# Router of a two-branch decoder layer with experts: squares beside the additions, a shorter root, second choice by weights, ranks as two sums, fewer fillers

## The chip, the cores and the metric

The kernel runs on one core of one Trainium2 chip. The metric is the device time of a launch in microseconds, as the median of several runs. A profile is of one execution; its own time stands beside the medians.

## What is computed

One layer for 256 tokens of width 2048, float32. A mixer (a state-space branch and an attention branch, gated and added) gives `x`; then a router picks for each token one of 4 groups and two of its 8 experts, and 32 experts of width 512 do their part:

```python
x = x + merged @ w_out[l]
h2 = rms_norm(x, ffn_norm_g[l])

g_prob = softmax(t @ rg_w + rg_b)                      # 4 groups, top 1
g_top, g_idx = lax.top_k(g_prob, 1)
e_logits = (t @ re_w + re_b).reshape(n_tok, 4, 8)[arange(n_tok), g_idx[:, 0]]
e_prob = softmax(e_logits)                             # 8 experts, top 2
e_top, e_idx = lax.top_k(e_prob, 2)
e_top = e_top / sum(e_top)
gate = g_top * e_top
for e in range(32):
    hid = silu(t @ w_gate[e]) * (t @ w_up[e])
    out = out + combine[:, e:e + 1] * (hid @ w_down[e])
```

## The kernel before

**Stages.** Up to some 625 us the kernel computes the mixer: weight blocks of 128 x 1024 are loaded (`raw`), split into a rounded part and a rest (`wh`, `wl`), and multiplied in three products each. The last four blocks are the output projection `wout`; `out_fin(n)` adds its result to `x2` (512 columns, two token halves t = 0 and 1), `x2_tr` transposes `x2` on TensorE (TensorE writes `bga`, ScalarE copies it to `xt2`) and takes the squares for the norm (`junk`, sums in `ssq`), `route_mm` multiplies with the router's weights (`wrg`). Transposes and router products are put off by some turns (`later`), so they come between the products of the next block; behind the last block (n = 3) they stand bare.

**Router.** Behind the last block come fillers, transposes of the identity that nobody reads (`keep_busy`, counts in `WARM`), then on VectorE the norm `r2` (`rsqrt`: ScalarE's root, a reciprocal and one Newton step), the logits `lgs`, and `first_max`: the maximum, a mask of those equal to it, the mask weighted with 8 to 1 (`desc`), the maximum of that, and a mask of the first. It is done for the experts of every group (`oh1`) and for the groups (`oh_g`, spread as `ohb`), in turns; then again for the second choice (`oh2`) with the first masked off (`el2`). `R1`, `R4` and `R32` (one name, `R`, in the profile, with 128x2, 128x8 and 128x64 elements) hold these values. A sum over the tokens (TensorE, with a triangle of ones `ult` and with `ones`) gives each token its rank in its expert (`rk`, in `bgb`), and from it the slot `slotv`.

**Experts.** An expert takes up to 32 tokens. For four experts at a time `gather` builds a selection (`EQ`, scaled as `SL`) and multiplies `x2` with it into `XB` (part of the tile `XY`); for the first four it is cut into pieces between the products of expert 0. `gate_up` uses four 2 MB pieces of weights (`ew`), `down` two. 192 pieces go through a ring of 11, later 10, buffers: `load_piece` issues the next when a buffer is free. Seven pieces are issued during the output projection, one near its end, three as soon as the mixer's buffers are free; every further one follows the use of a piece:

```python
            used[0] += 1
            load_piece()
```

**Order.** Each engine runs its instructions in the order in which the code issues them; nothing reorders them. All loads of weights are issued by SP, one queue, and a load that waits for its buffer holds up those behind it. Compute calls go through a helper, so all have line L77 in the profile; tiles tell them apart. Constants lie in one pool (`cp`), allocated ahead of the mixer's buffers and of three of the ring's.

Of the kernel before, what the change touches and what calls it, by code (L numbers as in the profile page):

```python
# [9 lines left out]
F32 = mybir.dt.float32  # L10
F32R = mybir.dt.float32r
I32 = mybir.dt.int32
AF = mybir.ActivationFunctionType
OP = mybir.AluOpType
# [3 lines left out]
P = 128  # L18
T = 256
D = 2048  # L20
EPS = 1e-6
# [17 lines left out]
LSPLIT = 512  # L39
NEG = -1.0e30  # L40
MAGIC = 12582912.0
WARM = (36, 8)


class Meter:
# [37 lines left out]
def hybrid_block(ctx, tc, A, out):  # L83
    nc = tc.nc
    load = {"vec": 0.0, "act": 0.0, "pe": 0.0}
    vec = Meter(nc.vector, load, "vec")
    act = Meter(nc.scalar, load, "act")
# [8 lines left out]
    def slot(h, shape, dt, name):  # L96
        return hp.tile(shape, dt, name=name, tag=f"h{h}")
# [13 lines left out]
    def bg_tile(k):  # L111
        return pbg.tile([P, 512], F32, name="bg" + "ab"[k], tag="bg" + "ab"[k])
# [66 lines left out]
    pool.iota(eidx, pattern=[[1, 1]], base=0, channel_multiplier=1, allow_small_or_imprecise_dtypes=True)  # L179
    iotan = cp.tile([P, 32], F32, name="iotan")  # L180
    vec.tensor_scalar(iotan, iota, -BIG, None, op0=OP.add)
    desc = cp.tile([P, 8], F32, name="desc")
    vec.tensor_scalar(desc, iota[:, 0:8], -1.0, 8.0, op0=OP.mult, op1=OP.add)

    def rsqrt(y, v, t):
        act.activation(t, v, AF.Sqrt)
        vec.reciprocal(y, t)
        vec.tensor_tensor(t, y, y, op=OP.mult)
        vec.tensor_tensor(t, t, v, op=OP.mult)
        vec.tensor_scalar(t, t, -0.5, 1.5, op0=OP.mult, op1=OP.add)  # L190
        vec.tensor_tensor(y, y, t, op=OP.mult)
# [173 lines left out]
    def out_fin(n):  # L365
        def f(a):
            c = slice(512 * n, 512 * n + 512)
            x2 = S["x2"]
            if n == 0:
                S["xt2"] = {}  # L370
                S["lg"] = [bg_tile(1), bg_tile(1)]
            for t in range(2):
                vec.tensor_tensor(x2[:, t, c], x2[:, t, c], a[t], op=OP.add)
            for t in range(2):
                later(D_X2 if n < 3 else 1, lambda t=t: x2_tr(n, t))
            for t in range(2):
                later(D_ROUTE if n < 3 else 2, lambda t=t: route_mm(n, t))
        return f

    def x2_tr(n, t):  # L380
        ps = bg_tile(0)
        for i in range(4):
            k = 4 * n + i
            pe.transpose(ps[:, P * i:P * i + P], S["x2"][:, t, P * k:P * k + P], ident)
        xt = S["xt2"][n, t] = slot((2 * n + t) % 4, [P, 4, P], F32, "xt2")
        act.copy(xt, ps.rearrange("p (i c) -> p i c", i=4))
        junk = slot(4 + (2 * n + t) % 4, [P, 512], F32, "junk")
        xs = S["x2"][:, t, 512 * n:512 * n + 512]
        if n < 3:
            act.activation(junk, xs, AF.Square, accum_out=ssq[:, t, n:n + 1])  # L390
            if n == 2 and t == 1:
                act.activation(tiny, ones[:, 0:1], AF.Sqrt)
        else:
            vec.scalar_tensor_tensor(junk, xs, 1.0, xs, op0=OP.mult, op1=OP.mult, accum_out=ssq[:, t, n:n + 1])
# [576 lines left out]
    def keep_busy(n):  # L971
        ps = acc_tile()
        for _ in range(n):
            pe.transpose(ps[:, 0:P], ident, ident)

    keep_busy(WARM[0])
    r2 = cp.tile([P, 4, 2], F32, name="r2")
    vec.tensor_reduce(r2[:, 0], ssq, axis=AX.X, op=OP.add)
    vec.tensor_scalar(r2[:, 1], r2[:, 0], 1.0 / D, EPS, op0=OP.mult, op1=OP.add)
    rsqrt(r2[:, 2], r2[:, 1], r2[:, 3])  # L980
    rs2 = r2[:, 2]
    lg = rt.tile([P, 2, 36], F32, name="lgs")
    for t in range(2):
        vec.scalar_tensor_tensor(lg[:, t], S["lg"][t][:, 0:36], rs2[:, t:t + 1], rbias, op0=OP.mult, op1=OP.add)
# [3 lines left out]
    OV = rt.tile([32, 35], F32, name="OV")  # L988
    oli = rt.tile([1, 33], I32, name="oli")

    def first_max(oh, x, m, one, wide):
        n, bc = x.shape[-1], lambda a: a.to_broadcast(list(x.shape))
        ds = desc[:, None, None, 8 - n:8] if wide else desc[:, None, 8 - n:8]
        ex = lambda a: bc(a[:, :, :, None] if wide else a[:, :, None])
        vec.tensor_reduce(m, x, axis=AX.X, op=OP.max)
        yield
        vec.tensor_tensor(oh, x, ex(m), op=OP.is_equal)
        yield
        vec.tensor_tensor(oh, oh, bc(ds), op=OP.mult)
        yield  # L1000
        vec.tensor_reduce(one, oh, axis=AX.X, op=OP.max)
        yield
        vec.tensor_tensor(oh, oh, ex(one), op=OP.is_equal)
        yield

    gl = lg[:, :, 0:4]
# [8 lines left out]
            lambda: act.activation(gx, gx, AF.Exp),  # L1015
            lambda: vec.tensor_tensor(oh1, oh1, ohb, op=OP.mult)]
    vec.scalar_tensor_tensor(el2, oh1, NEG, el, op0=OP.mult, op1=OP.add)
    for i, _ in enumerate(first_max(oh2, el2, m2, R4[:, 4], True)):
        if i < len(side):
            side[i]()  # L1020
    vec.tensor_tensor(oh2, oh2, ohb, op=OP.mult)
    dif, w1, w2_ = R4[:, 5], R4[:, 6], R4[:, 7]
    vec.tensor_tensor(R32[:, 3], oh1, oh2, op=OP.add)
    vec.tensor_tensor(dif, m2, m1, op=OP.subtract)
    act.activation(dif, dif, AF.Exp)
    M = R32[:, 3].rearrange("p t g e -> p t (g e)")
    rk = bg_tile(1)
    pe.matmul(rk[:, 0:64], ult, R32[:, 3].rearrange("p t g e -> p (t g e)"), start=True, stop=False)
    pe.matmul(rk[:, 32:64], ones, M[:, 0], start=False, stop=True)
    keep_busy(WARM[1])  # L1030
    gsum = R1[:, 1]
    vec.tensor_reduce(gsum, gx, axis=AX.X, op=OP.add)
    rank = rk[:, 0:64].rearrange("p (t e) -> p t e", t=2)
# [258 lines left out]
```

## Time and profile before

| | us |
|---|---|
| Median of 3 runs | 1555.99 (1554.79 to 1556.02) |
| The profiled execution | 1556.73 |
| Its span, first to last instruction | 1555.0 |
| TensorE busy in the span | 1256.5 (81%) |
| VectorE busy | 541.9 (35%) |
| ScalarE busy | 450.9 (29%) |
| Chain that ended last: DMA, TensorE, VectorE, ScalarE | 51%, 46%, 2%, 1% |

The shares are means over two stages that have different limits, so they are read by stretch: the mixer up to 625 us, the router up to 635 us, the experts behind it. A timeline row gives start, duration and the idle time of the engine before it with what ended it; "x2" after a shape counts instructions merged into the row. A float32 matmul stands as two instructions there.

### The profile page before, as it was taken

Reading aid. Unit: us, or ns where it says so; the run is one execution under the profiler, and the core shown is the slowest. Engines: PE = TensorE matmul, PEld = TensorE weight load, DVE = VectorE, ACT = ScalarE, POOL = GpSimd, SP = SyncE. Lnnn points to the kernel's source line nnn. Section 1 sums busy time; section 2 is a strip of 40 time slices with the busy share of each in tenths; the row PEclk is TensorE's granted clock in tenths of the full one; section 3 lists DMA queues with packets and bytes.
Section 4 is the critical chain, followed back from the end, with each engine's and each line's share of the span. In section 5 each row is a group of like instructions: output and inputs, shape, how many; then the busy total and the mean of one; then the engine's idle time right before and its main releaser. Section 6 shows DMA issues by size and latency. Waiting matters only on the chain.

```text
span 1555.0 us, 25114 instructions
## 1 busy us (share of the span) xinstructions
PE 1256.5 (81%) x10646; PEld 857.4 (55%) x10646; DVE 541.9 (35%) x1346; ACT 450.9 (29%) x768; POOL 49.4 (3%) x105
## 2 busy tenths in 40 slices
PE   9999999999999999878558558558657657657697
PEld 8888888888878888644224224224224223324364
DVE  7846787898866644302002002002002002002001
ACT  5654576644454444211101101100110110110101
POOL 6600000000000000000000000000000000000000
PEclk9999999999999999999779879879789778979999
DMA  8645555566658877999999999999999999999996
GB/s 266 200 141 167 176 159 172 154 195 194 192 179 298 270 277 245 382 429 426 427 427 427 427 427 428 426 428 428 426 428 427 427 426 429 426 427 429 426 427 235
DMA packets 65106, 516.90 MB, mean 332 GB/s; under 512 B 7904, under 2 KB 8160, under 8 KB 41440
## 3 DMA queue, kind: packets, MB, share of 16 engines
q1 hardware_dynamic: 64704, 515.21, 84.4%
q8 instruction: 85, 1.39, 0.4%
q14 instruction: 29, 0.24, 0.0%
q10 hardware_dynamic: 288, 0.06, 0.0%
HBM read 513.14 MB, written 2.10 MB: 331 GB/s over the span
## 4 chain that ended last, share of the span: by engine, by line
DMA 51%; PE 46%; DVE 2%; ACT 1%; issue 0%; SPq 0%; DVEq 0%
PE acc L77 41%; DMA ew<-wgu 30%; DMA ew<-wd 20%; PE bga L77 3%; PE bgb L77 2%; ACT XY L77 0%; DMA raw<-win 0%; DVE R L77 0%; ACT wh L77 0%; DVE wl L77 0%; DVE Vs L77 0%; ACT AT L77 0%; DVE prod L77 0%; ACT uy L77 0%; DVE rtmp L77 0%
## 5 line engine op out<-in xcount | busy, mean ns | idle before, releaser
L77 PE MATMUL acc<-ew,XY 128*32 128x256 f32 x4096 | 310.3, 456 | 166.2 <-DMA ew<-wgu 166.2
L77 PEld LDWEIGHTS acc<-ew,XY 128*32 128x32 f32 x4096 | 142.2, 126 | 318.5 <-DMA ew<-wgu 182.0
L77 DVE TENSOR_TENSOR wl<-raw,wh 128x1024 fp32r<-128x1024 f32 (+1 forms) x201 | 244.1, 1218 | 138.8 <-ACT wh L77 137.6
L77 ACT CAST wh<-raw 128x1024 fp32r<-128x1024 f32 x199 | 208.5, 1052 | 177.1 <-PE acc L77 118.6
L77 DVE TENSOR_TENSOR sg<-sg,acc 128x128 f32<-128x128 f32 x32 | 9.2, 288 | 653.1 <-ACT sg L77 653.1
L77 PE MATMUL acc<-ew,hT 128*32 128x256 f32 (+1 forms) x2080 | 149.4, 437 | 73.2 <-DMA ew<-wd 41.8
L77 ACT COPY XY<-acc 32x256 f32<-32x256 f32 (+1 forms) x260 | 93.6, 360 | 213.6 <-PE acc L77 211.1
L77 PEld LDWEIGHTS acc<-ew,hT 128*32 128x32 f32 x2080 | 73.7, 123 | 138.3 <-issue 59.9
L77 PE MATMUL acc<-wh,xh 128*128 128x512 f32 x512 | 145.2, 400 | 0.8 <-ACT wh L77 0.6
L77 PE MATMUL acc<-wh,xl 128*128 128x512 f32 x512 | 140.2, 390 | 0.0
L77 PE MATMUL acc<-wl,xh 128*128 128x512 f32 x512 | 140.0, 390 | 0.0
L77 ACT ACTIVATE sg<-acc 128x128 f32<-128x128 f32 x32 | 8.9, 278 | 413.9 <-PE acc L77 413.9
L77 PEld LDWEIGHTS acc<-wh,xl 128*128 128x128 f32 x512 | 96.5, 188 | 20.8
L77 PEld LDWEIGHTS acc<-wl,xh 128*128 128x128 f32 x512 | 96.4, 188 | 20.4
L77 PEld LDWEIGHTS acc<-wh,xh 128*128 128x128 f32 x512 | 93.7, 190 | 20.4 <-ACT wh L77 1.4
L77 DVE TENSOR_TENSOR Vs<-Vs,prod 128x32 f32<-128x32 f32 x508 | 76.9, 222 | 0.0
L77 PE MATMUL acc<-XY,sc 128*128 128x512 f32 x128 | 64.5, 647 | 14.5 <-ACT XY L77 14.5
L77 PE MATMUL bga<-SL,x 128*128 128x128 f32 x512 | 63.5, 280 | 10.3 <-DVE SL L77 10.3
L77 PEld LDWEIGHTS bga<-SL,x 128*128 128x128 f32 x512 | 59.0, 192 | 22.9 <-DVE SL L77 15.9
L77 DVE TENSOR_TENSOR accv<-accv,acc 128x512 f32<-128x512 f32 x56 | 38.5, 688 | 86.7 <-PE acc L77 86.7
L77 PE MATMUL acc<-wh,m 128*128 128x512 f32 x256 | 64.6, 392 | 0.0
L77 DVE TENSOR_TENSOR prod<-Vs,coef 128x64 f32<-128x64 f32 x254 | 56.0, 262 | 0.0
(224 smaller groups left out, 975.3 us busy)
## 6 DMA issues: line engine op xcount, KB each, us to landing
ew<-wgu SPq DMA_DIRECT2D x123, 2048.0 KB, 39.1
ew<-wd SPq DMA_DIRECT2D x61, 2048.0 KB, 39.1
raw<-win SPq DMA_DIRECT2D x127, 512.0 KB, 4.1
raw<-wout SPq DMA_DIRECT2D x32, 512.0 KB, 4.1
ew<-wgu SPq DMA_DIRECT2D x20, 512.0 KB, 5.9
raw<-wba SPq DMA_DIRECT2D x16, 512.0 KB, 4.6
raw<-wbs SPq DMA_DIRECT2D x16, 512.0 KB, 5.1
raw<-wglu SPq DMA_DIRECT2D x8, 512.0 KB, 5.2
```

The costliest lines, as they stand in the source:

```text
L77: return f(out, *args, **kw)
```

## The change

Five edits, all in the router. The squares of the last 512 columns (`x2_sq`) are issued right behind each addition, not behind the transposes. The root takes scale and offset in its own instruction, from the sum, while the scaled sum is computed beside it for the Newton step, whose four instructions become three. For the second choice the tie-break weights are first multiplied with the group mask (`dsg`), so that the mask `oh2` comes out with its group and needs no product behind it; its last comparison takes the larger of 0.5, so that zeros never match. The ranks are summed from `oh1` and from `oh2` apart, two matmuls each into the same sums, where before they were summed from the addition of both. The fillers are 22, 3 and 8 instead of 36 and 8. A constant `epst` is new.

```diff
--- before.py
+++ after.py
@@ -39,7 +39,7 @@
 LSPLIT = 512
 NEG = -1.0e30
 MAGIC = 12582912.0
-WARM = (36, 8)
+WARM = (22, 3, 8)
 
 
 class Meter:
@@ -179,6 +179,8 @@
     pool.iota(eidx, pattern=[[1, 1]], base=0, channel_multiplier=1, allow_small_or_imprecise_dtypes=True)
     iotan = cp.tile([P, 32], F32, name="iotan")
     vec.tensor_scalar(iotan, iota, -BIG, None, op0=OP.add)
+    epst = cp.tile([P, 1], F32, name="epst")
+    vec.memset(epst, EPS)
     desc = cp.tile([P, 8], F32, name="desc")
     vec.tensor_scalar(desc, iota[:, 0:8], -1.0, 8.0, op0=OP.mult, op1=OP.add)
 
@@ -371,6 +373,8 @@
                 S["lg"] = [bg_tile(1), bg_tile(1)]
             for t in range(2):
                 vec.tensor_tensor(x2[:, t, c], x2[:, t, c], a[t], op=OP.add)
+                if n == 3:
+                    x2_sq(n, t)
             for t in range(2):
                 later(D_X2 if n < 3 else 1, lambda t=t: x2_tr(n, t))
             for t in range(2):
@@ -384,6 +388,10 @@
             pe.transpose(ps[:, P * i:P * i + P], S["x2"][:, t, P * k:P * k + P], ident)
         xt = S["xt2"][n, t] = slot((2 * n + t) % 4, [P, 4, P], F32, "xt2")
         act.copy(xt, ps.rearrange("p (i c) -> p i c", i=4))
+        if n < 3:
+            x2_sq(n, t)
+
+    def x2_sq(n, t):
         junk = slot(4 + (2 * n + t) % 4, [P, 512], F32, "junk")
         xs = S["x2"][:, t, 512 * n:512 * n + 512]
         if n < 3:
@@ -976,9 +984,13 @@
     keep_busy(WARM[0])
     r2 = cp.tile([P, 4, 2], F32, name="r2")
     vec.tensor_reduce(r2[:, 0], ssq, axis=AX.X, op=OP.add)
+    rs2, nt = r2[:, 2], r2[:, 3]
+    act.activation(nt, r2[:, 0], AF.Sqrt, scale=1.0 / D, bias=epst)
     vec.tensor_scalar(r2[:, 1], r2[:, 0], 1.0 / D, EPS, op0=OP.mult, op1=OP.add)
-    rsqrt(r2[:, 2], r2[:, 1], r2[:, 3])
-    rs2 = r2[:, 2]
+    vec.reciprocal(rs2, nt)
+    vec.scalar_tensor_tensor(nt, rs2, -0.5, rs2, op0=OP.mult, op1=OP.mult)
+    vec.tensor_tensor(nt, nt, r2[:, 1], op=OP.mult)
+    vec.scalar_tensor_tensor(rs2, nt, 1.5, rs2, op0=OP.add, op1=OP.mult)
     lg = rt.tile([P, 2, 36], F32, name="lgs")
     for t in range(2):
         vec.scalar_tensor_tensor(lg[:, t], S["lg"][t][:, 0:36], rs2[:, t:t + 1], rbias, op0=OP.mult, op1=OP.add)
@@ -988,7 +1000,7 @@
     OV = rt.tile([32, 35], F32, name="OV")
     oli = rt.tile([1, 33], I32, name="oli")
 
-    def first_max(oh, x, m, one, wide):
+    def first_max(oh, x, m, one, wide, mask=None):
         n, bc = x.shape[-1], lambda a: a.to_broadcast(list(x.shape))
         ds = desc[:, None, None, 8 - n:8] if wide else desc[:, None, 8 - n:8]
         ex = lambda a: bc(a[:, :, :, None] if wide else a[:, :, None])
@@ -996,11 +1008,15 @@
         yield
         vec.tensor_tensor(oh, x, ex(m), op=OP.is_equal)
         yield
-        vec.tensor_tensor(oh, oh, bc(ds), op=OP.mult)
+        vec.tensor_tensor(oh, oh, bc(ds) if mask is None else mask, op=OP.mult)
         yield
         vec.tensor_reduce(one, oh, axis=AX.X, op=OP.max)
         yield
-        vec.tensor_tensor(oh, oh, ex(one), op=OP.is_equal)
+        if mask is None:
+            vec.tensor_tensor(oh, oh, ex(one), op=OP.is_equal)
+        else:
+
+            vec.scalar_tensor_tensor(oh, oh, 0.5, ex(one), op0=OP.max, op1=OP.is_equal)
         yield
 
     gl = lg[:, :, 0:4]
@@ -1015,19 +1031,27 @@
             lambda: act.activation(gx, gx, AF.Exp),
             lambda: vec.tensor_tensor(oh1, oh1, ohb, op=OP.mult)]
     vec.scalar_tensor_tensor(el2, oh1, NEG, el, op0=OP.mult, op1=OP.add)
-    for i, _ in enumerate(first_max(oh2, el2, m2, R4[:, 4], True)):
+    dsg = R32[:, 4]
+    vec.tensor_tensor(dsg, ohb, desc[:, None, None, :].to_broadcast([P, 2, 4, 8]), op=OP.mult)
+    rk = bg_tile(1)
+    M4 = R32[:, 3]
+    M = M4.rearrange("p t g e -> p t (g e)")
+
+    def ranks(oh, first):
+        pe.matmul(rk[:, 0:64], ult, oh.rearrange("p t g e -> p (t g e)"), start=first, stop=False)
+        pe.matmul(rk[:, 32:64], ones, oh.rearrange("p t g e -> p t (g e)")[:, 0], start=False, stop=not first)
+
+    for i, _ in enumerate(first_max(oh2, el2, m2, R4[:, 4], True, dsg)):
         if i < len(side):
             side[i]()
-    vec.tensor_tensor(oh2, oh2, ohb, op=OP.mult)
+    ranks(oh1, True)
+    keep_busy(WARM[1])
+    ranks(oh2, False)
+    keep_busy(WARM[2])
     dif, w1, w2_ = R4[:, 5], R4[:, 6], R4[:, 7]
-    vec.tensor_tensor(R32[:, 3], oh1, oh2, op=OP.add)
+    vec.tensor_tensor(M4, oh1, oh2, op=OP.add)
     vec.tensor_tensor(dif, m2, m1, op=OP.subtract)
     act.activation(dif, dif, AF.Exp)
-    M = R32[:, 3].rearrange("p t g e -> p t (g e)")
-    rk = bg_tile(1)
-    pe.matmul(rk[:, 0:64], ult, R32[:, 3].rearrange("p t g e -> p (t g e)"), start=True, stop=False)
-    pe.matmul(rk[:, 32:64], ones, M[:, 0], start=False, stop=True)
-    keep_busy(WARM[1])
     gsum = R1[:, 1]
     vec.tensor_reduce(gsum, gx, axis=AX.X, op=OP.add)
     rank = rk[:, 0:64].rearrange("p (t e) -> p t e", t=2)
```

On VectorE, from the last output additions (`x`) to the logits (`lgs`), before:

```order
L77 TENSOR_TENSOR x_4612<-x_4612,acc 128x512 x2
L77 SCALAR_TENSOR_TENSOR junk,ssq<-x_4612 128x512 x2
L77 TENSOR_REDUCE r_5991<-ssq 128x2
L77 TENSOR_SCALAR r_5991<-r_5991 128x2
L77 RECIPROCAL r_5991<-r_5991 128x2
L77 TENSOR_TENSOR r_5991<-r_5991 128x2 x2
L77 TENSOR_SCALAR r_5991<-r_5991 128x2
L77 TENSOR_TENSOR r_5991<-r_5991 128x2
L77 SCALAR_TENSOR_TENSOR lgs<-bgb,r_5991,rbias 128x36 x2
```

and with the change (`r` is `r2`; numbers are buffers and mean nothing else):

```order
L77 TENSOR_TENSOR x_4614<-x_4614,acc 128x512
L77 SCALAR_TENSOR_TENSOR junk,ssq<-x_4614 128x512
L77 TENSOR_TENSOR x_4614<-x_4614,acc 128x512
L77 SCALAR_TENSOR_TENSOR junk,ssq<-x_4614 128x512
L77 TENSOR_REDUCE r_5979<-ssq 128x2
L77 TENSOR_SCALAR r_5979<-r_5979 128x2
L77 RECIPROCAL r_5979<-r_5979 128x2
L77 SCALAR_TENSOR_TENSOR r_5979<-r_5979 128x2
L77 TENSOR_TENSOR r_5979<-r_5979 128x2
L77 SCALAR_TENSOR_TENSOR r_5979<-r_5979 128x2
L77 SCALAR_TENSOR_TENSOR lgs<-bgb,r_5979,rbias 128x36 x2
```

A square now stands between the additions, and one instruction less between the reciprocal and `lgs`.

On VectorE, the second choice, from the masking of the first (reads `lgs`) to the slots (read `bgb`), before:

```order
L77 SCALAR_TENSOR_TENSOR R_6005<-R_6005,lgs 128x64
L77 TENSOR_REDUCE R_6004<-R_6005 128x8
L77 TENSOR_TENSOR R_6004<-lgs,R_6003 128x8
L77 TENSOR_TENSOR R_6005<-R_6005,R_6004 128x64
L77 TENSOR_TENSOR R_6005<-R_6005,desc 128x64
L77 TENSOR_TENSOR R_6005<-R_6005,R_6004 128x64
L77 TENSOR_REDUCE R_6004<-R_6005 128x8
L77 TENSOR_TENSOR R_6005<-R_6005,R_6004 128x64 x2
L77 TENSOR_TENSOR R_6005<-R_6005 128x64
L77 TENSOR_TENSOR R_6004<-R_6004 128x8
L77 TENSOR_REDUCE R_6003<-R_6004 128x2
L77 SCALAR_TENSOR_TENSOR R_6005<-R_6005,bgb 128x64
```

and with the change, from the instruction behind that masking:

```order
L77 TENSOR_TENSOR R_5992<-R_5991,desc 128x64
L77 TENSOR_REDUCE R_5991<-R_5992 128x8
L77 TENSOR_TENSOR R_5991<-lgs,R_5990 128x8
L77 TENSOR_TENSOR R_5992<-R_5992,R_5991 128x64
L77 TENSOR_TENSOR R_5992<-R_5992 128x64
L77 TENSOR_TENSOR R_5992<-R_5992,R_5991 128x64
L77 TENSOR_REDUCE R_5991<-R_5992 128x8
L77 SCALAR_TENSOR_TENSOR R_5992<-R_5992,R_5991 128x64
L77 TENSOR_TENSOR R_5992<-R_5992 128x64
L77 TENSOR_TENSOR R_5991<-R_5991 128x8
L77 TENSOR_REDUCE R_5990<-R_5991 128x2
L77 SCALAR_TENSOR_TENSOR R_5992<-R_5992,bgb 128x64
```

The product with `desc` has moved to the front, and the comparison is the last instruction on `oh2`; what stands behind it is the addition, the difference for the gates and a sum.

On TensorE, from the last router products to the first gather (`SL`), before:

```order
L77 MATMUL bgb<-wrg,xt_5918 128x36 x4
L77 MATMUL bgb<-wrg,xt_5927 128x36 x4
L77 MATMUL acc<-ident 128x128 x36
L77 MATMUL bgb<-R_6005,ult 128x64
L77 MATMUL bgb<-R_6005,ones 128x32
L77 MATMUL acc<-ident 128x128 x8
L77 MATMUL bga<-SL,x_4612 128x128 x8
```

and with the change:

```order
L77 MATMUL bgb<-wrg,xt_5924 128x36 x4
L77 MATMUL bgb<-wrg,xt_5931 128x36 x4
L77 MATMUL acc<-ident 128x128 x22
L77 MATMUL bgb<-R_5992,ult 128x64
L77 MATMUL bgb<-R_5992,ones 128x32
L77 MATMUL acc<-ident 128x128 x3
L77 MATMUL bgb<-R_5992,ult 128x64
L77 MATMUL bgb<-R_5992,ones 128x32
L77 MATMUL acc<-ident 128x128 x8
L77 MATMUL bga<-SL,x_4614 128x128 x8
```

Two rank sums stand where there was one, with three fillers between them, and fewer fillers ahead.

## Rows read from the trace of the kernel before

**Rows 1.** Busy time by stretch: us, busy time by engine, granted clock, DMA share, GB/s.

```profile
634.00:657.00 23.00, 19.04 (x240) 13.03 (x238) 6.55 (x23) 3.15 (x7) 0.00 (x0) 1.00 0.92 362
657.00:1480.00 823.00, 543.10 (x6171) 276.21 (x6171) 74.30 (x141) 103.23 (x299) 0.00 (x0) 0.85 1.01 427
```

**Rows 2.** Chain of waits, end of the stream: start, duration, what.

```profile
1440.07 40.62 DMA ew<-wd
1480.82 22.14 PE acc L77 x256
```

**Rows 3.** Timeline of the load queue (SP): start, duration, what was issued.

```profile
638.69 0.33 SPq L885 DMA_DIRECT2D ew<-wd  x1
644.32 0.33 SPq L885 DMA_DIRECT2D ew<-wgu  x1
```

**Rows 4.** Busy time by stretch, behind the first issue of rows 3.

```profile
638.00:640.00 2.00, 2.00 (x24) 1.57 (x17) 0.00 (x0) 0.00 (x0) 0.00 (x0) 1.00 0.54 123
640.00:642.00 2.00, 2.00 (x20) 2.00 (x19) 0.69 (x1) 0.00 (x0) 0.00 (x0) 1.00 0.74 295
```

**Rows 5.** Timeline of VectorE (DVE): start, duration, operation, idle before and releaser.

```profile
624.07 0.69 DVE L77 TENSOR_TENSOR x<-x,acc 128x512 f32<-128x512 f32 x1 [5.20 <-PE acc L77]
625.44 0.69 DVE L77 TENSOR_TENSOR x<-x,acc 128x512 f32<-128x512 f32 x1 [0.68 <-PE acc L77]
626.65 0.69 DVE L77 SCALAR_TENSOR_TENSOR junk<-x 128x512 f32<-128x512 f32 x1
627.38 0.16 DVE L77 TENSOR_REDUCE r<-ssq 128x2 f32<-128x8 f32 x1
628.02 0.17 DVE L77 RECIPROCAL r<-r 128x2 f32<-128x2 f32 x1 [0.27 <-ACT r L77]
629.09 0.42 DVE L77 SCALAR_TENSOR_TENSOR lgs<-bgb,r,rbias 128x36 f32<-128x36 f32 x2
```

**Rows 6.** Timeline of ScalarE (ACT), last copies and the root.

```profile
626.88 0.59 ACT L77 COPY xt<-bga 128x512 f32<-128x512 f32 x1 [0.42 <-PE bga L77]
627.78 0.20 ACT L77 ACTIVATE r<-r 128x2 f32<-128x2 f32 x1 [0.32 <-DVE r L77]
```

**Rows 7.** Timeline of TensorE (PE), fillers, ranks, first gather.

```profile
628.43 4.13 PE L77 MATMUL acc<-ident 128*128 128x128 f32 x36
632.92 0.43 PE L77 MATMUL bgb<-R,ult 128*128 128x64 f32 x2 [0.37 <-DVE R L77]
633.19 0.36 PE L77 MATMUL bgb<-R,ones 128*128 128x32 f32 x2
633.39 1.07 PE L77 MATMUL acc<-ident 128*128 128x128 f32 x8
634.74 1.46 PE L77 MATMUL bga<-SL,x 128*128 128x128 f32 x11 [0.28 <-DVE SL L77]
```

**Rows 8.** Timeline of VectorE, second choice.

```profile
630.83 0.22 DVE L77 SCALAR_TENSOR_TENSOR R<-R,lgs 128x64 f32<-128x64 f32 x1
631.09 0.22 DVE L77 TENSOR_REDUCE R<-R 128x8 f32<-128x64 f32 x1
631.74 0.22 DVE L77 TENSOR_TENSOR R<-R,R 128x64 f32<-128x64 f32 x1
632.12 0.49 DVE L77 TENSOR_TENSOR R<-R,R 128x64 f32<-128x64 f32 x2
632.64 0.30 DVE L77 TENSOR_TENSOR R<-R 128x64 f32<-128x64 f32 x2
```

**Rows 9.** TensorE behind a pause, and its clock: a timeline row, a stretch.

```profile
703.21 3.40 PE L77 MATMUL acc<-ew,hT 128*32 128x256 f32 x32 [2.01 <-DMA ew<-wd]
...
704.00:706.00 2.00, 2.00 (x27) 0.50 0.93 393
```

**Rows 10.** DMA issues: what, count, size of one, median us to landing.

```profile
BC<-bc SPq DMA_DIRECT2D x4, 256.0 KB, 5.3
wrg<-wr SPq DMA_DIRECT2D x1, 288.0 KB, 5.5
```

## The prediction

> **What bounds the kernel now.** I read first the busy time by stretches of the run. From 657 to 1480 us the DMA engines are busy all the time at 427 GB/s, TensorE only 543 of 823 us, and in 634 to 657 us the DMA share is 0.92 [rows 1]. The expert stage is thus a stream of weight loads; whatever happens on the compute engines in it costs nothing unless it holds up a load. The chain of waits says how the stream reaches the end: a load of `ew` that ends at 1480.69 us releases TensorE, which then works in one row towards the end [rows 2]. So a microsecond by which the whole stream comes earlier is a microsecond of the run, and one in which the stream is not held up is worth nothing.
>
> The change lies ahead of the stream, between the last output addition (625.44 us) and the first gather (634.74 us). Does that stretch hold the stream up? The load queue answers: the twelfth piece is issued at 638.69 us, the next at 644.32 us [rows 3]. Each of them waits until TensorE has used up a quarter of expert 0's weights, which can't begin before the router has chosen the tokens. In the two windows behind that first issue the DMA share is 0.54 and 0.74 [rows 4]: 0.46 x 2 + 0.26 x 2 = 1.44 us in which the DMA engines had nothing to do. Both issues, and all that follow until the stream is full, hang on the router's end. So the first 1.4 us taken off the router pass to the end of the run one for one; more would have to come out of the smaller holes in 642 to 657 us.
>
> **The last squares.** Before, VectorE does both additions and then both squares; the second square begins at 626.65, the sum over `ssq` at 627.38 us, 0.73 later [rows 5]. Now the first square stands between the additions. The first addition runs from 624.07 for 0.69 us, so its square can begin at about 624.80 (0.04 lie between the end of the second square, 627.34, and the sum that depends on it) and is done by 625.49, against 625.44 for the second addition, which waits for TensorE until then [rows 5]: 0 to 0.05 us late, and the idle time of VectorE covers the square. The second square follows its own addition: 625.44 + 0.69 + 0.04 = 626.17, and the sum 0.73 later, 626.90. That is 0.48 us earlier (0.43 at worst). If the cover failed, the transposes of `x2` would be late by what the addition is.
>
> **The root straight from the sum.** Before: sum 627.38, the scaling, root on ScalarE at 627.78 [rows 5, 6], so 0.20 per step. Now ScalarE takes scale and offset into the root, and the scaling runs on VectorE beside it: one step less, so the root's input is there at 626.90 + 0.20 = 627.10. But ScalarE isn't free then: the copy of the last `xt2` begins at 626.88 and lasts 0.59 us [rows 6], and stands ahead of the root in its queue. It hangs on the transposes, which the change doesn't bring forward. So the root begins at 627.49, not 627.10: of 0.48 + 0.20 = 0.68 us only 627.78 - 627.49 = **0.29 us** arrive; the rest turns into a wait for the copy. Were the copy and the root overlapped, up to 0.68 would arrive; I take the copy's whole duration, since the row gives it.
>
> From the reciprocal to the first `lgs` there are four instructions in 1.07 us [rows 5]; now there are three, at 0.20 a step: **0.20 us**. `lgs` begins at 629.09 - 0.49 = 628.60. Next late would be the router's own matmuls: the fillers behind them begin at 628.43 [rows 7], so `lgs` finds them done, with little to spare.
>
> **The second choice.** The new product (`dsg`) goes between the masking of the first choice (630.83) and the maximum that depends on it (631.09) [rows 8]. Two independent instructions of this size take 0.30 us together, a dependent one starts 0.26 after its forerunner [rows 8]; so it fits in a gap and costs 0, or 0.04 at worst. At the end the group mask of the second choice and the addition of the two masks leave the path: 632.12, two instructions in dependence, then the pair at 632.64, then TensorE at 632.92 [rows 7, 8]. Three steps become one: the second choice could be at TensorE at 632.12 + 0.28 = 632.40, 0.52 us earlier.
>
> **Ranks as two sums.** But TensorE is then not free either. The masked first choice (631.74) reaches TensorE 0.28 later, 632.02; its two rank matmuls occupy 633.39 - 632.92 = 0.47 us, and the three fillers behind them 3 x 4.13 / 36 = 0.34 us [rows 7, 8]. The queue is in order, so the second sum begins at 632.83, not 632.40. It ends 0.63 later (632.92 to 633.19 + 0.36) [rows 7], 0.09 us earlier than now; if its first weights are loaded under the fillers, up to 0.2 us more. I take **0.15 us** out of 0.09 to 0.29. Without the three fillers it would be some 0.3 us more. The addition of the masks is still needed for the slots, but falls into that wait.
>
> **Fewer fillers.** 36 fillers of 0.115 us end at 632.56, shortly before the ranks; 22 end at 630.96, and the first choice arrives (0.49 us early) at 631.53. TensorE stands idle for 0.57 us where it now does for 0.37. The fillers aren't on the path; what they are worth is the clock, a rival below. The layout moves too: the new 4-byte constant `epst` takes 32 bytes and shifts all that is allocated behind it.
>
> **The sum.** 0.29 + 0.20 + 0.15 = 0.64 us, within 1.44 us of idle DMA, so all of it reaches the end; the bounds are 0.5 (0.29 + 0.20 + 0.09 less 0.09 for a late addition and for `dsg`) and 1.2 (0.68 + 0.20 + 0.29). The profiled execution took 1556.73 us (its span is 1555.0): 1556.73 - 0.64 = 1556.09. The median of the runs shown is 0.74 lower, 1555.99, and gives 1555.35. They spread over 1.2 us, twice the gain. A measurement of this kernel can tell about 0.2% (3.1 us) from no change; so I forecast a gain that is real but too small to be seen.
>
> **The rivals.** (1) The wait only moves: copy and fillers take the whole gain, or the DMA queue's holes behind 642 us keep it. Then 1556.0. For it: both new waits above are of that kind. Against: the terms are counted behind them.
> (2) All the hunger of the stream goes. In 634 to 657 us it moved 362 GB/s instead of 427 [rows 1], which is 23 x 65 / 427 = 3.5 us of lost transfer. If an earlier start let all of it go: 1552.5, faster by over 0.2%. Against: the router gives back 0.64 us, and TensorE, at 19.04 of 23 us busy, paces the releases there.
> (3) TensorE falls to half its clock in the first gather, for want of fillers. After an idle time of 2.01 us the granted clock was 0.50 (1.2 GHz) in the window from 704 us [rows 9]. TensorE paces the loads from 634.74 on [rows 7], so each us at half clock costs 0.5 us; it decides, slower by over 0.2%, from (3.1 + 0.64) / 0.5 = 7.5 us of it. If the whole gather up to 648 us ran at half, some 14 us, the time would be 1555.35 + 7 = 1562.4. Against: in 634 to 657 us TensorE was idle for 4 of 23 us and kept 1.00 (2.4 GHz) [rows 1], and the new pause is 0.57 us.
> (4) The shift by 32 bytes makes loads slower. Three of the ten buffers of the stream lie behind `epst`, on a 64-byte boundary before and off it now: 0.3 x 823 = 247 us of the stream, so each per cent costs 2.5 us and it decides from 1.5%; at 2% the time would be 1560.3. Against: `wrg` lay off such a boundary all along, and its 288 KB landed in 5.5 us where the 256 KB of `BC`, on one, took 5.3 [rows 10]. By size 6.0 would be expected, so no loss shows, though a single load resolves no per cent.
> The Trainium skill speaks for a small loss of this kind: "DMA: Bandwidth & Descriptors", section "How a descriptor splits into AXI transactions", says that a transaction has to start at a 256-byte boundary and that the bytes ahead of the descriptor's start cost beats of 32 bytes. The section tells it of reads; no row here shows it for writes into these buffers. If it holds for them, a 16 KB row that starts 160 instead of 128 bytes behind such a boundary takes one beat more in some 516, an estimate by that page of 0.2% of 247 us or 0.5 us, and the time would be 1555.8.
>
> **How the numbers follow.** My forecast (1554.8 to 1555.5) 0.67; the gain lost in moved waits, or eaten by a small shift cost (1555.6 to 1556.3) 0.17; all the hunger gone or another gain of that size 0.05; half clock 0.05, of which 0.02 stays under 0.2%; the shift at over 1.5% 0.05, or at less 0.01. So faster 0.05, same 0.87, slower 0.08. The range adds the spread of the runs to the forecast and the first rival and ends short of the large cases: 1553.8 to 1557.6.
>
> **What would show it.** Right: the root on ScalarE begins right behind the copy of `xt2`; `lgs` comes about 0.5 us earlier against the last addition; the second rank sum starts right behind three fillers; the first gather, and with it the twelfth piece, 0.6 us earlier; DMA share in the two windows up by a fourth to a half of the hole. Wrong: a granted clock under 1.00 in 634 to 657 us (rival 3), under 427 GB/s in the full stream (rival 4), a root that begins under the copy (the gain is nearer to 1.0), or a second addition that starts well after the last matmul.

## The result, and the profile after

The changed kernel takes **1565.43 us** (median of 6 runs, 1564.25 to 1566.79), the kernel before 1554.93 us (6 runs, 1554.20 to 1556.02) on the same chip: a ratio of 1.0066, interval 1.0056 to 1.0076. That is 10.5 us slower, where 0.6 us faster was forecast. The profiled execution took 1565.38 us with a span of 1563.7 us. The spans differ by 8.7 us only, since the profiled execution of before lay 1.8 us over its median.

The diff touches the router alone, so the router is read first. VectorE from the last additions on, in the kernel after (start, duration, operation, idle before with its releaser):

```profile
633.88 0.69 DVE L77 TENSOR_TENSOR x<-x,acc 128x512 f32<-128x512 f32 x1 [5.50 <-PE acc L77]
634.60 0.69 DVE L77 SCALAR_TENSOR_TENSOR junk<-x 128x512 f32<-128x512 f32 x1
635.28 0.69 DVE L77 TENSOR_TENSOR x<-x,acc 128x512 f32<-128x512 f32 x1
636.00 0.69 DVE L77 SCALAR_TENSOR_TENSOR junk<-x 128x512 f32<-128x512 f32 x1
636.74 0.16 DVE L77 TENSOR_REDUCE r<-ssq 128x2 f32<-128x8 f32 x1
637.53 0.17 DVE L77 RECIPROCAL r<-r 128x2 f32<-128x2 f32 x1 [0.43 <-ACT r L77]
638.40 0.42 DVE L77 SCALAR_TENSOR_TENSOR lgs<-bgb,r,rbias 128x36 f32<-128x36 f32 x2
...
640.14 0.23 DVE L77 SCALAR_TENSOR_TENSOR R<-R,lgs 128x64 f32<-128x64 f32 x1
640.28 0.22 DVE L77 TENSOR_TENSOR R<-R,desc 128x64 f32<-128x64 f32 x1
640.42 0.21 DVE L77 TENSOR_REDUCE R<-R 128x8 f32<-128x64 f32 x1
```

ScalarE there, the copy of the last `xt2` and the root:

```profile
636.72 0.58 ACT L77 COPY xt<-bga 128x512 f32<-128x512 f32 x1 [0.41 <-PE bga L77]
637.20 0.30 ACT L77 ACTIVATE r<-r,epst 128x2 f32<-128x2 f32 x1
```

TensorE from the fillers to the first gather, less the second sum's other half:

```profile
638.27 2.60 PE L77 MATMUL acc<-ident 128*128 128x128 f32 x22
641.34 0.43 PE L77 MATMUL bgb<-R,ult 128*128 128x64 f32 x2 [0.47 <-DVE R L77]
641.61 0.36 PE L77 MATMUL bgb<-R,ones 128*128 128x32 f32 x2
641.81 0.53 PE L77 MATMUL acc<-ident 128*128 128x128 f32 x3
642.17 0.33 PE L77 MATMUL bgb<-R,ult 128*128 128x64 f32 x2
...
643.88 1.35 PE L77 MATMUL bga<-SL,x 128*128 128x128 f32 x10 [0.28 <-DVE SL L77]
```

Measured as a distance from the last addition, which is how a stage is read when all ahead of it has moved, the router became shorter. From the last addition to the gather: 634.74 - 625.44 = 9.30 us before [rows 5, 7], 643.88 - 635.28 = **8.60 us** after. So 0.70 us were saved, against 0.64 forecast. But the last addition itself starts at 635.28 instead of 625.44 us [rows 5]: **9.84 us late, before the first changed instruction runs.**

Behind the router nothing was lost. The stretch of the first gather and the full stream, after (us, busy time by engine, granted clock, DMA share, GB/s), to be set beside [rows 1]:

```profile
643.80:666.80 23.00, 20.29 (x231) 13.37 (x235) 5.93 (x21) 2.20 (x4) 0.00 (x0) 0.87 0.94 368
666.80:1488.00 821.20, 544.45 (x6183) 277.92 (x6175) 74.23 (x141) 102.45 (x297) 0.00 (x0) 0.85 1.01 427
```

The stream moves 427 GB/s as before. From the first gather to the end of the span are 1563.7 - 643.88 = 919.82 us, before 1555.0 - 634.74 = 920.26 us. The account of the spans: +9.84 (mixer) - 0.70 (router) - 0.44 (experts) = +8.70 us.

**Where in the mixer?** Comparing the same event in both traces shows where the distance grows:

| event | before, us | after, us | late by |
|---|---|---|---|
| ScalarE's first copy of `qk`, begin | 76.25 | 76.36 | 0.1 |
| first gate | 234.16 | 236.88 | 2.7 |
| attention projection (products with `ya`), begin | 312.83 | 316.86 | 4.0 |
| attention projection, its last result taken | 356.68 | 360.72 | 4.0 |
| gate, next branch | 377.08 | 381.72 | 4.6 |
| gate, three blocks later | 442.36 | 448.92 | 6.6 |
| addition of output block n = 0 | 550.63 | 558.70 | 8.1 |
| n = 1 | 575.12 | 583.89 | 8.8 |
| n = 2 | 600.14 | 608.97 | 8.8 |
| n = 3, second half | 625.44 | 635.28 | 9.8 |

It is no single wait: the distance grows with nearly every block of weights, but not at all in the attention projection. Between the two gates a block's price can be read. ScalarE's gates before, then after (the idle time in brackets is ScalarE's):

```profile
377.08 0.69 ACT L77 ACTIVATE gate<-acc,rstd 128x512 f32<-128x512 f32 x1 [1.21 <-PE acc L77]
442.36 0.69 ACT L77 ACTIVATE gate<-acc,rstd 128x512 f32<-128x512 f32 x1 [0.35 <-PE acc L77]
```

```profile
381.72 0.69 ACT L77 ACTIVATE gate<-acc,rstd 128x512 f32<-128x512 f32 x1 [1.29 <-PE acc L77]
448.92 0.69 ACT L77 ACTIVATE gate<-acc,rstd 128x512 f32<-128x512 f32 x1 [0.48 <-PE acc L77]
```

Three blocks hold 288 products of 512 columns: (442.36 - 377.08) / 288 = 65.28 / 288 = **226.7 ns** each before, (448.92 - 381.72) / 288 = 67.20 / 288 = **233.3 ns** after. The same products, on the same engine, are 6.7 ns (2.9%) slower. It is not the clock. Busy time by stretch, within these blocks, before and after (columns as in [rows 1]):

```profile
380.00:440.00 60.00, 60.00 (x266) 49.67 (x266) 53.21 (x203) 25.82 (x27) 0.00 (x0) 1.00 0.67 210
```

```profile
380.00:440.00 60.00, 60.00 (x259) 48.20 (x258) 50.37 (x195) 26.30 (x28) 0.00 (x0) 1.00 0.65 200
```

TensorE is busy all of 60 us and granted the full clock in both; it starts 259 products where it started 266, 2.6% fewer (rows may lack a few records). The groups by tile say which ones. TensorE's products with the rest `wl`, before (count, busy us, mean ns of one, idle; the mean is from start to end of one product, longer than the distance between two, since they overlap):

```profile
L77 PE MATMUL acc<-wl,xh 128*128 128x512 f32 x512 | 140.0, 390 | 0.0
...
L77 PE MATMUL acc<-wl,ys 128*128 128x512 f32 x64 | 17.8, 389 | 0.0
L77 PE MATMUL acc<-wl,ya 128*128 128x512 f32 x64 | 17.8, 389 | 0.0
L77 PE MATMUL acc<-zz,wl 128*128 128x256 f32 x64 | 9.0, 283 | 0.0
```

and after:

```profile
L77 PE MATMUL acc<-wl,xh 128*128 128x512 f32 x512 | 142.6, 395 | 0.0
...
L77 PE MATMUL acc<-wl,ys 128*128 128x512 f32 x64 | 18.2, 395 | 0.0
L77 PE MATMUL acc<-wl,ya 128*128 128x512 f32 x64 | 17.8, 389 | 0.0
L77 PE MATMUL acc<-zz,wl 128*128 128x256 f32 x64 | 8.9, 281 | 0.0
```

Products that hold `xh` (the activations' rounded part; `xl` is its rest) or `ys` and stream a weight tile went from 389 or 390 to 395 ns, those with `m` likewise; those that hold `ya` stayed at 389; the 256-column ones, in which the weights are held and `zz` streams, rather became faster.

**What these have in common is an address.** The constant `epst` takes 32 bytes in its pool. All that is allocated behind that pool moves by 32 bytes: `raw`, `wh`, `wl`, the small buffers `ya`, `qkT`, `xt2`, and, once the mixer is done, the router's tiles and three of the stream's buffers. What is allocated ahead of it (`xh`, `xl`, `m`, `ys`, `zz`, the other buffers of the stream) stays. Before, all the operands named started 128 bytes past a multiple of 512, by the kernel's own allocation. After, a product with `xh` holds a tile that starts there and streams one that starts 32 bytes further on; in a product with `ya` both start 32 bytes further on. 2112 products of 512 columns hold a tile that stayed (1536 with `xh` or `xl`, 384 with `m`, 192 with `ys`); at 6.7 ns each this would be 14 us. 9.84 us arrive. One part of the rest is 192 products that lose nothing: those of the first two weight blocks, up to 53 us, which hold every second column of `xh` or `xl` (`slice(t, T, 2)` in the code). TensorE there, before, then after:

```profile
22.20 1.09 PE L77 MATMUL acc<-wh,xl 128*128 128x512 f32 x4
...
39.00 1.09 PE L77 MATMUL acc<-wh,xl 128*128 128x512 f32 x4
```

```profile
21.93 1.10 PE L77 MATMUL acc<-wh,xl 128*128 128x512 f32 x4
...
38.73 1.10 PE L77 MATMUL acc<-wh,xl 128*128 128x512 f32 x4
```

From the first of the two rows to the second are 18 rows of four products, 72 in all, and 16.80 us in both kernels: 233.3 ns each, in the kernel before as in the one after, and as much as a misplaced pair takes. So the table shows no loss up to 76 us. From there to the first gate the starts are some 5 ns further apart, since they are at 228 ns before; what is then still missing was not followed up.

### The profile page after: what moved, and what is told of

It is laid out like the page before. It is cut to its first block, busy times and chain, and to the rows that moved or that the text cites. A ratio compares the mean times of both kernels' runs of the same rounds, so it can differ in the third digit from the quotient of the medians.

```text
span 1563.7 us, 25100 instructions
## 1 busy us (share of the span) xinstructions
PE 1267.7 (81%) x10639; PEld 856.4 (55%) x10639; DVE 542.2 (35%) x1346; ACT 450.3 (29%) x768; POOL 49.9 (3%) x105
## 5 line engine op out<-in xcount | busy, mean ns | idle before, releaser
L77 PE MATMUL acc<-ew,hT 128*32 128x256 f32 (+1 forms) x2080 | 153.7, 446 | 77.3 <-DMA ew<-wd 48.6
```

Of the source, the lines that this page charges most:

```text
L77: return f(out, *args, **kw)
```

## The experiments

Three theories were to be told apart: (A) the shift makes the mixer's products slower; (B) it makes loads into the three shifted buffers of the stream slower, the prediction's fourth rival; (C) the new instructions do harm by themselves. Within A: (A1) what counts is where the streamed tile lies, (A2) what counts is the difference between the two operands. All kernels compute the whole layer. "Products" below is the mean of the group that holds `xh` and streams `wl`. The expectations count in rows of four weight loads instead (TensorE loading the tile that it holds): such a row in the mixer's blocks lasts 0.87 us before and 0.89 us after.

**e1_level80** puts the mixer's buffers back and leaves everything else of the change. The mixer's pool of constants has a tile, `level`, that nothing reads; 32 bytes less of it cancel those of `epst`. The router's tiles and the three buffers of the stream stay shifted. The run was to tell A from B and C.

```diff
-    cq.tile([P, 88], F32, name="level")
+    cq.tile([P, 80], F32, name="level")
```

> The changed kernel, with an unused tile in the mixer's pool cut from 88 to 80 words, so that raw, wh, wl and the slots of xt2, ya and qkT lie where they lay before the change; epst, the router's tiles and three of the ring's buffers stay 32 bytes further. If the loss comes from the mixer's buffers lying 32 bytes further, TensorE's 512-column products go back to 0.87 us for a row of four weight loads, the last output addition to about 625.4 us, and only the router's gain of 0.7 us is left: about 1554.2 us, ratio to before 0.9995. If the three shifted ring buffers cost the time (the rival of the prediction), or the new instructions do, it stays at about 1565 us.

Measured: 1555.05 us (11 runs) against 1555.35 us (21 runs), ratio 0.9996, interval 0.9987 to 1.0005. The loss is gone. Its products, and its full stream by busy time:

```profile
L77 PE MATMUL acc<-wl,xh 128*128 128x512 f32 x512 | 140.0, 390 | 0.0
```

```profile
657.00:1479.00 822.00, 543.11 (x6174) 276.77 (x6171) 74.28 (x141) 102.84 (x298) 0.00 (x0) 0.85 1.01 427
```

The products are at 390 ns again; the last addition is at 625.65, the gather at 634.25 us, so the router keeps its 8.60 us; and the stream runs at 427 GB/s into buffers that are still shifted. B and C fall.

**e2_pad32** is the kernel before with the constant alone: a tile that nothing writes or reads.

```diff
+    cp.tile([P, 1], F32, name="epst")
     desc = cp.tile([P, 8], F32, name="desc")
```

> The kernel before, with 32 bytes reserved in the pool of constants where the change puts epst, and no other edit. If the shift alone makes the loss, it is the loss of the changed kernel plus the router's 0.7 us: about 1566.1 us, 11 us over before, with rows of four weight loads at 0.89 us in the mixer. If the changed instructions make it: 1554.9 us.

Measured: 1566.27 us (4 runs) against 1555.35, ratio 1.0063, interval 1.0048 to 1.0079. Not one instruction was added or moved, and the whole loss is there: last addition at 635.17 us, router at the old 9.30 us.

```profile
L77 PE MATMUL acc<-wl,xh 128*128 128x512 f32 x512 | 142.7, 395 | 0.0
```

**e4_all32** and **e6_units32** separate A1 from A2. e4 is before with 32 bytes ahead of all pools, those of `xh`, `m` and `ys` included, so that every operand lies 32 bytes further on. e6 has the same and takes 32 bytes from `level`, so that `wh`, `wl` and `ya` are back on their old places and only `xh`, `xl`, `m`, `ys` are shifted.

```diff
+    ctx.enter_context(tc.tile_pool(name="pad", bufs=1)).tile([P, 8], F32, name="pad")
     U = {i: ctx.enter_context(tc.tile_pool(name=f"u{i}", bufs=1)) for i in range(11) if i != 6}
```

> The kernel before, with 32 bytes reserved ahead of everything, so that the held operands (xh, xl, m, ys, ya) and the streamed weights (wh, wl) are shifted alike: all lie 32 bytes behind a 64-byte boundary. If what counts is that the two operands of a product lie at a different place within 64 bytes, nothing changes: about 1554.9 us. If what counts is that the streamed tile lies off a 64-byte boundary: about 1565 us or more, the products with ya slow too.

> The kernel before, with 32 bytes reserved ahead of everything and the unused tile cut from 88 to 80 words, so that wh, wl, raw and ya stay on their places and the held operands xh, xl, m and ys move 32 bytes off the 64-byte boundary. If the difference within 64 bytes counts: slow as the change, about 1565 us, products with ya at 0.87 us for four, the others at 0.89. If the streamed tile's own boundary counts: about 1554.9 us.

Measured: e4 1555.57 us (10 runs), ratio 1.0000, interval 0.9991 to 1.0009; e6 1564.55 us (4 runs), ratio 1.0057, interval 1.0042 to 1.0073, both against 1555.35. Products of e4, then of e6:

```profile
L77 PE MATMUL acc<-wl,xh 128*128 128x512 f32 x512 | 140.1, 390 | 0.0
L77 PE MATMUL acc<-wl,ya 128*128 128x512 f32 x64 | 17.8, 389 | 0.0
```

```profile
L77 PE MATMUL acc<-wl,xh 128*128 128x512 f32 x512 | 143.1, 396 | 0.0
L77 PE MATMUL acc<-wl,ya 128*128 128x512 f32 x64 | 17.8, 390 | 0.0
```

e4 streams from shifted tiles and loses nothing; e6 streams from the old places and loses nearly all (last addition 634.57 us). So neither tile's own place counts, but the difference of the two: A2.

**e3_pad64** is the kernel after with a shift of 64 bytes instead of 32.

```diff
-    epst = cp.tile([P, 1], F32, name="epst")
+    epst = cp.tile([P, 9], F32, name="epst")[:, 0:1]
```

> The changed kernel with epst in a tile of 36 bytes, which takes 64 in the pool, so that all behind it moves by 64 bytes instead of 32. If the place within 64 bytes is what counts, the mixer is as fast as before and the router's 0.7 us remain: about 1554.6 us where before is 1555.3. If the distance of the two operands counts over a larger unit (128 bytes or more), it is slow: about 1565 us, or some other loss.

Measured: 1558.00 us (10 runs) against 1555.71 (21 runs), ratio 1.0013, interval 1.0003 to 1.0022, last addition at 627.78 us. That 64 bytes would be free was wrong: they make the last addition 2.3 us late (627.78 - 625.44), where 32 bytes made it 9.8 us late.

```profile
L77 PE MATMUL acc<-wl,xh 128*128 128x512 f32 x512 | 140.9, 392 | 0.0
```

**e5_hp32** is before with 32 bytes at the head of the pool of small buffers, so that of the operands only `ya`, `qkT` and `xt2` move: if A2 holds, the roles change, and the products with `ya` alone become slower. It has a single run.

```diff
+    hp.tile([P, 8], F32, name="hpad", tag="hpad")
```

> The kernel before, with 32 bytes reserved at the head of the pool that holds ya, qkT and xt2, so that of all held operands only ya moves against wh and wl. If the difference of the operands counts: the 192 products with ya lose 6.3 ns each, 1.2 us, and show 0.89 us for four weight loads, while those with xh, xl, m and ys stay at 0.87; about 1556.5 us. If the streamed tile's boundary counts: no product is slower.

```profile
L77 PE MATMUL acc<-wl,xh 128*128 128x512 f32 x512 | 140.2, 391 | 0.0
L77 PE MATMUL acc<-wl,ya 128*128 128x512 f32 x64 | 18.2, 396 | 0.0
```

The roles did change: 396 ns for `ya`, 391 for `xh`. The attention projection's products took 1.26 us longer in all, which is 6.6 ns for each of the 192, the same price as above. Its one time, 1559.62 us, is more than that explains: the last addition came at 627.17 us, 1.7 late, and from the gather to the end it took 921.33 us, 1.1 more than before. Its granted clock was 0.95 from 100 to 600 us, a little under the upper level (2.4 GHz), where every other profile here has 1.00. Whether that is the rest, a single run does not settle.

**e8_off16** is before with `wh` and `wl` in tiles that are 16 words longer and used from an offset of four words on, meant as a difference of 16 bytes. It too has a single run.

```diff
+OFF = 4
...
+    def split_tiles():
+        return tuple(wp.tile([P, 1040], F32R, name=n, tag=n)[:, OFF:OFF + 1024].rearrange("p (k c) -> p k c", k=2)
+                     for n in ("wh", "wl"))
...
-        h = wp.tile([P, 2, 512], F32R, name="wh", tag="wh")
-        l = wp.tile([P, 2, 512], F32R, name="wl", tag="wl")
+        h, l = split_tiles()
```

> The kernel before, with wh and wl in tiles of 4160 bytes of which the 4096 behind the first 16 are used, so that the streamed operand lies 16 bytes behind a 64-byte boundary and the held ones on it. If any difference within 64 bytes costs, four weight loads of the mixer take 0.89 us and the time is about 1565 us; if only the other half of 64 bytes costs, 0.87 us and about 1555.3.

```profile
L78 PE MATMUL acc<-wl,xh 128*128 128x512 f32 x512 | 142.1, 394 | 0.0
```

One time of 1564.39 us, last addition at 633.12 us, and 0.96 us over the 192 products with `ya`, 5 ns each. But the run is not one of a single difference. The longer tiles take 4160 bytes, 64 more than a multiple of 512, and each of the two has three buffers: modulo 512 the streamed operand lies 16, 80 or 144 bytes (`wh`) and 208, 272 or 336 bytes (`wl`) behind `xh`, `m` and `ys`, and 144 to 464 behind `ya`. All of these are 16 bytes past a multiple of 64. Sorted by buffer, the starts in the mixer's trace are 231.2 to 232.7 ns apart on average for each of the six, 231.4 at 16 bytes, where the same average is 227.4 before. So every one of these differences costs 4 to 5 ns, a little less than 32 bytes and more than 64.

**e7_nomid** is for the prediction's side remark on the router: e1 without the three fillers between the rank sums, which were to hold up the second sum by some 0.3 us.

```diff
-WARM = (22, 3, 8)
+WARM = (22, 0, 8)
...
     ranks(oh1, True)
-    keep_busy(WARM[1])
     ranks(oh2, False)
```

> The changed kernel with the unused tile at 80 words (mixer's buffers on their old places) and without the three fillers between the two rank sums. By the prediction's account of TensorE's queue the second rank sum then starts when the second choice is there, some 0.3 us earlier, and the first gather begins about 8.3 us behind the last output addition instead of 8.6 (9.3 in the kernel before): about 1554.3 us where before is 1555.3. If the fillers held nothing up, 8.6.

TensorE and the last addition in it:

```profile
624.96 0.69 DVE L77 TENSOR_TENSOR x<-x,acc 128x512 f32<-128x512 f32 x1
```

```profile
631.48 0.41 PE L77 MATMUL bgb<-R,ult 128*128 128x64 f32 x2
...
633.27 0.91 PE L77 MATMUL bga<-SL,x 128*128 128x128 f32 x6 [0.28 <-DVE SL L77]
```

From the last addition to the gather 633.27 - 624.96 = 8.31 us, 0.29 less than with them. The time is 1554.57 us (11 runs) against 1555.71, ratio 0.9993, interval 0.9984 to 1.0002: the lowest median of the versions run, and still not to be told from the kernel before.

## Why the prediction was wrong

**The step that failed** is the last sentence of "Fewer fillers": "The layout moves too: the new 4-byte constant `epst` takes 32 bytes and shifts all that is allocated behind it." It is right, and it went into the sum at nothing. The fourth rival then asked for the price in one place only, the loads into the stream's three shifted buffers, and gave it a chance of 0.05 at 1560.3 us. The same shift moves `raw`, `wh` and `wl`, and TensorE streams from the latter two for most of 550 us. The part on what bounds the kernel placed the change between the last output addition and the first gather, and no term or rival covers the mixer ahead of it; but a change of address needs no instruction. In the trace of before nothing shows a misplaced pair, since all these tiles start alike, so its price could not have been read there; but its leverage could have been stated. What the runs showed in place of nothing is 9.84 us in the mixer: 5 to 6.7 ns on each product whose two operands no longer start alike. From 76 us to the last addition TensorE sets the pace (it is busy in 548.5 of the 549 us up to 625), some 550 us, so each per cent on its matmuls is 5.5 us, and with the gain of 0.64 us it decides at (3.1 + 0.64) / 5.5 = 0.7%. The rival bounded the same shift in a stage of 247 us and missed the one of 550.

**The fourth rival as written** was wrong: loads into shifted buffers show no loss. The stream moves 427 GB/s in both kernels [rows 1], the sign that the prediction named for it, and e1 has the shifted buffers at a ratio of 0.9996. The prediction's estimate by the Trainium skill, "DMA: Bandwidth & Descriptors", section "How a descriptor splits into AXI transactions", was 0.5 us more; this is 0.03%, and e1's interval reaches 0.05% above 1, so it neither bears out nor excludes it.

**The router's terms** held, as a distance from the last addition:

| term | forecast, us | measured, us |
|---|---|---|
| sum and root, up to the root's start (2.34 to 1.92) | 0.29 | 0.42 |
| root to `lgs` | 0.20 | 0.11 |
| `lgs` to gather (5.65 to 5.48) | 0.15 | 0.17 |
| together | 0.64 | 0.70 |

- The first square is covered as foreseen: the second addition starts at 635.28, 0.68 behind the square's start, with no idle ahead of it, while TensorE's last product had just ended (635.25), 0.03 earlier; before, 0.04 lay between the two. So nothing was late.
- The root did **not** wait for the whole copy: it starts at 637.20, the copy ends at 637.30. The prediction named this overlap as the upper bound's reason and did not take it; 0.10 of the 0.13 us too little is that. The root needed its input at 636.74 + 0.20 = 636.94 at the earliest, so ScalarE was the later one, as argued.
- The root itself takes 0.30 us instead of 0.20 [rows 6], and the reciprocal starts 0.33 us behind it instead of 0.24 [rows 5, 6]. That is a cost not foreseen, 0.09 us, of the root's new form: it applies a scale, and an offset that it reads from `epst`. No run has one of them alone. From the reciprocal to `lgs` are 0.87 instead of 1.07 us: the 0.20 forecast, of which 0.11 is left with it.
- `dsg` cost 0.02 us: 640.14, 640.28, 640.42, so the maximum starts 0.28 behind the masking, 0.26 before [rows 8].
- The second rank sum starts at 642.17 right behind the three fillers; e7 confirms the price of them, 0.29 us against "some 0.3".

**Whether the gain reaches the end.** The twelfth and thirteenth pieces of the stream are issued 12.55 and 18.18 us behind the last addition, 13.25 and 18.88 before [rows 3, 5]: 0.70 earlier both times. The load queue after, and two windows at its first issue:

```profile
647.83 0.33 SPq L893 DMA_DIRECT2D ew<-wd  x1
```

```profile
647.00:649.00 2.00, 2.00 (x27) 1.50 (x20) 0.00 (x0) 0.00 (x0) 0.00 (x0) 1.00 0.70 221
649.00:651.00 2.00, 2.00 (x20) 2.00 (x20) 0.69 (x1) 0.00 (x0) 0.00 (x0) 1.00 0.81 295
```

The hole is (0.30 + 0.19) x 2 = 0.98 us instead of 1.44 [rows 4], a third less, within the fourth to a half that the prediction named; but these are 0.46 us for 0.70 us of router, so that the gain passes on one for one is seen at the queue and not in the hole. The span of e1 is 0.6 us shorter than before's (1554.4 against 1555.0): 0.21 late at the last addition, 0.70 from the router, 0.11 behind the gather. That of e7 is 2.4 shorter (1552.6), of which 0.99 is the router; the rest, 0.48 ahead of it and 0.93 behind, no edit explains. The medians of e1 and e7, 0.3 and 1.1 us under those of before, point the same way, but both intervals hold 1. So the gain is traced as far as the load queue, and at the end of the run it is too small to be shown, as the prediction had said.

**The other rivals.** That the wait only moves (1) does not fit the 0.70 us at the load queue. That all hunger goes (2) did not come: 368 instead of 362 GB/s. Half clock (3) did come, a mean of 0.87 in the first 23 us of the gather, where before had 1.00; but not from the fillers. e4, with the old router and all its fillers, has it too; e7, with the fewest, has not, and e3, with those of the kernel after, has 1.00 in these 23 us. The first 23 us of the gather in e4, then in e7:

```profile
634.80:657.80 23.00, 20.30 (x227) 13.35 (x231) 5.92 (x21) 2.20 (x4) 0.00 (x0) 0.86 0.91 358
```

```profile
633.20:656.20 23.00, 18.68 (x239) 12.91 (x243) 5.91 (x21) 3.66 (x8) 0.00 (x0) 1.00 0.96 376
```

Nor did it cost what was forecast: a mean of 0.87 over 23 us is 0.13 x 23 / 0.5 = 6 us at half clock, 3 us at the end by the prediction's 0.5 us for each, and yet the kernel after needs 919.82 us from gather to end where before needs 920.26. Rows of the kernel after show where it lies:

```profile
658.00:660.00 2.00, 1.18 (x14) 0.77 (x18) 0.79 (x5) 1.50 (x2) 0.00 (x0) 1.00 1.10 426
...
662.00:664.00 2.00, 1.13 (x9) 0.18 (x1) 0.29 (x1) 0.41 (x2) 0.00 (x0) 0.50 0.99 393
664.00:666.80 2.80, 2.61 (x28) 1.21 (x32) 0.00 (x0) 0.14 (x1) 0.00 (x0) 0.50 1.01 427
```

The clock is full until 660 us and at half (1.2 GHz) from 662 us on, 18 us behind the start of the gather, behind a stretch in which TensorE was idle for 0.8 of 2 us. The loads go on at 393 and 427 GB/s there. The rival had priced half clock inside the first 14 us; there it did not come, so its price there is not shown.

## What to carry to other kernels

A new tile, however small, is a change to every stage whose buffers are allocated behind it: list those stages, and put a bound on each that is compute-bound, not only on the one that the edit is about. When a stage without an edited line becomes slower, compare the groups of instructions by tile in both traces; those that kept their duration (`ya` here) tell more than those that lost it. Then look at the addresses of both operands, and keep or adjust a tile that only fills space, like `level`, with each new constant.

## What was not expected of the hardware

- A product of 512 columns in the rounded float32 form takes 226.7 ns when the held and the streamed tile start at the same address modulo 512, and more with the differences that were tried: some 6.7 ns at 32 bytes (after, e2, e6, and with the roles changed e5), some 2 ns at 64 (e3), 4 to 5 ns at each of six from 16 to 336, all 16 past a multiple of 64 (e8, one run). When both are shifted alike (e4, 1.0000) it is free. The Trainium skill, "SBUF — State Buffer", section "Operand start alignment", asks only that an operand start at a multiple of its element size and says that its runs timed nothing; every tile here obeys it, and the time still differs.
- Where the held tile is read in every second column (the first two blocks), the products take 233.3 ns with tiles that start alike and with a shift of 32 bytes. Whether the second column is the reason, no run tells.
- The 256-column products with the weights held and `zz` streamed show the reverse in the groups, 283 to 281 ns. In the expert stage three of the stream's buffers are shifted against `XY`; its products (`acc<-ew,XY`) have a mean of 456 ns before and after, but that mean ranges from 452 to 462 ns over the runs, so a price of this size could not be seen there.
- Open: why TensorE loses time on a difference (no run shows the inside of a product), by what unit the difference counts, and the rest of e5's time. From first gather to end the executions spread from 918.6 to 921.3 us, more than the whole change to the router.
